# Projecting the first layer's memory values behind the routing instead of in the attention stage

## The chip, the cores and the metric

One core of a Trainium2 chip runs the whole kernel in one launch. The metric is the device time of that launch in microseconds (us). All data are float32.

## The reference

Two blocks run one after the other on 512 tokens of width 1024. The first is a block of sparse attention, a state-space mixer and 16 experts; the second runs two layers (DEPTH_2 = 2), each with a recurrent and windowed-attention mixer, a cross attention to a memory of 256 rows (`mem`), and a swiglu. Cut to what matters here:

```python
def first_block(x, ...):
    att = dsa_attention(q, k, v, iq, ik, iw * INDEXER_SCALE, topk)
    ssd = ssd_mixer(z, xbc, dt_raw, ...)
    mixed = jnp.einsum('bse,ed->bsd', jnp.concatenate([att, ssd], -1), w_out[l])
    x = layer_norm(ALPHA * x + mixed, ln1_g[l], ln1_b[l])
    ffn = hier_moe(x, w_route_group[l], b_route_group[l], w_route_expert[l], ...)
    return layer_norm(ALPHA * x + ffn, ln2_g[l], ln2_b[l])

def hier_moe(h, w_rg, b_rg, w_re, b_re, w_gate, w_up, w_down):
    p_group = jax.nn.softmax((h @ w_rg + b_rg).astype(f32), -1)
    ...
    for e in range(N_EXPERTS):
        hid = jax.nn.silu(h @ w_gate[e]) * (h @ w_up[e])
        y = y + gates[..., e:e + 1] * (hid @ w_down[e])

def cross_attention(u, mem, cq_w, ckv_w, co_w):
    q = (u @ cq_w).reshape(B, S, CROSS_HEADS, CROSS_HEAD_DIM)
    k, v = jnp.split(mem @ ckv_w, 2, axis=-1)
    s = jnp.einsum('bshd,bmhd->bhsm', q, k).astype(jnp.float32) * (CROSS_HEAD_DIM ** -0.5)
    p = jax.nn.softmax(s, axis=-1)
    return jnp.einsum('bhsm,bmhd->bshd', p, v).reshape(B, S, CROSS_WIDTH) @ co_w
```

The product `mem @ ckv_w` of either layer depends on nothing that the first block computes. The kernel computes it early, keeps it in DRAM and reads it back in the layer that uses it.

## The kernel before

**Arithmetic.** A float32 product is made of three matmuls. Each operand is split into a high part (a copy to fp32r on ACT) and a low part (a subtraction on DVE, or on POOL): high x high, high x low, low x high. Tiles named `wh` and `wl` are the two parts of a piece of weights (128 x 1024 elements); `hTh`/`hTl` are those of the activations, transposed; `memh`/`meml` those of the memory.

**Order of the work.** The class `Plan` records every operation of the program first, then lists them in an order of its own: of the operations that are ready by its modelled costs it takes the one that stands first in the program, a little later work filling gaps. Nearly all instructions are therefore issued from one line, L338, and the order on each engine is fixed before the kernel runs; each engine then works through its queue strictly in that order. A `Stream` loads weights in items of 1 MB into two buffers named `raw` (SP issues these loads) and splits them into pieces that go to one of two rings of four, `ring` and `tail` (`take`, L560 to L593). The low part of a piece is made on DVE, except for the keys of the memory and two early projections (L593): those are made on POOL. PSUM banks have three tags with 3, 3 and 2 banks (L208). The projections here use those with tag m.

**The stages around the change**, in the program's order:

- The attention stage: for each of four query blocks `ssd_chunk(i)`, `topk`, `attend(i)` (L1287 to L1291). The scores' softmax, its splits and the products with the values (tiles `pt`, `pth`, `ptl`, `vh`, `vl`) depend on each other, so that PE needs other work in between. `CKV[0]` names such work (L1292): pieces of `ckv`.
- `ckv(l, part)` (L1262 to L1285) projects a part of layer l's memory keys and values. Part "k" makes the keys: eight units of 24 matmuls 128x256, tile `ck`. Parts "0" and "1" make one half of the values each: four pieces of weights, two token tiles, 48 matmuls 128x512, tile `cv`. A result goes from PSUM to an SBUF tile (`kept`, `cko`) and from there to DRAM (`kd`, `vd`).
- The projection `wo` with the norm: 192 matmuls 128x512 in two halves of the columns, four token tiles each; the input x (tile `htokb`, loaded by POOL's queue once the pools of the attention are closed) is added, and the norm's result is transposed to `hTh`, `hTl`.
- The routing: `route()` (the router's matmuls, a long chain of small instructions on DVE, `Lg` to `w`), then for each of the 16 experts its `slots` (a 128x512 comparison on DVE, then eight small matmuls `slot` and `gate` on PE) that give an index list `idx`. `CKV[1]` follows `route()` in the program (L1673).
- The experts: for each of 16, an indirect DMA on POOL's queue gathers its tokens (`xg<-hd,idx`, L1687), PE transposes them (`ps<-ca,xg`), then gate and up (`gu`, 2 MB of weights) and down (1 MB). Three tiles `xg` take the gathers in turn. The loads for several experts run ahead into whatever buffers are free.
- `CKV[2]` follows the experts (L1804). The values of the first layer are read back in the second block, near 985 us.

```python
CKV = (((0, "k"), (0, "0"), (0, "1")), ((1, "k"),), ((1, "0"), (1, "1")))
        plan.critical = True
        route()
        plan.critical = False
        for x in CKV[1]:
            ckv(*x)
```

Of the kernel before, what the change touches and what calls it, by code (L numbers as in the profile page):

```python
# [202 lines left out]
LAT = {"PEACT": 197, "PEDVE": 197, "PEPool": 222, "PEPE": 0, "ACTACT": 153, "ACTDVE": 142, "ACTPE": 271, "ACTPool": 180,  # L203
       "DVEDVE": 127, "DVEACT": 128, "DVEPE": 202, "DVEPool": 153, "PoolPE": 203, "PoolPool": 120}
AHEAD = 50
CKV = (((0, "k"), (0, "0"), (0, "1")), ((1, "k"),), ((1, "0"), (1, "1")))
TABLE_SLACK = 60
PSUM_TAGS = {"m": 3, "c": 3, "s": 2}  # L208
SETS = {}
# [429 lines left out]
def body(tc, a, out):  # L639
# [5 lines left out]
    with ctx:  # L645
# [15 lines left out]
        def bank(name="ps", tag=None):  # L661
            tag = tag or ("c" if name == "ps" else "m")
            return psum.tile([P, 512], F32, tag=tag, name=name, bufs=PSUM_TAGS[tag])
# [60 lines left out]
        def ckv_items(l, part, raws=None, where="ring"):  # L724
            w = a["ckv_w_2"][l]
            if part == "k":
                feat_items(f"ck{l}", w, range(0, 1024))
            else:
                h = int(part)
                tok_items(f"cv{l}{h}", w, K8, 1024 + 512 * h, 512, where, raws=raws)  # L730

        for x in CKV[0]:
            ckv_items(*x)
        for h in range(2):
            tok_items(f"wo{h}", w_out, K8, h * 512, 512,
                      where=("ring", "tail")[h])
        for x in CKV[1]:
            ckv_items(*x)
# [39 lines left out]
        raws = ["raw", "raw", "raw2", "rawb"]  # L778
        for x in CKV[2]:
            ckv_items(*x, raws, "ring")  # L780
# [94 lines left out]
        def feat_mm(p, w, xh, xl, t0=0, t1=NT, kts=K8):  # L875

            wh, wl = w
            n, last = 0, 3 * len(kts) - 1
            o = p[:, t0 * 128:t1 * 128]
            for l, r in ((wh, xh), (wl, xh), (wh, xl)):  # L880
                for k in kts:
                    mm(o, l[:, k, :], r[:, t0:t1, k, :], kts[0] == 0 and n == 0, kts[-1] == 7 and n == last)
                    n += 1

        def tok_mm(p, w, xh, xl, t, kts, n, start, stop):

            wh, wl = w
            c, last = 0, 3 * len(kts) - 1
            for l, r in ((xh, wh), (xh, wl), (xl, wh)):
                for i, k in enumerate(kts):  # L890
                    mm(p[:, :n], l[:, t, k, :], r[:, i, :n], start and c == 0, stop and c == last)
                    c += 1
# [340 lines left out]
        def attend(i):  # L1233
            w = (i + 1) * P
            pts = []
            for pr in range(4):
                ps = pair_scores(hTh[:, i, pr, :], hTl[:, i, pr, :], kTh, kTl, w)
                pt = p3.tile([P, 2, S], F32, tag="pt", name=f"pt{i}_{pr}", bufs=5)[:, :, :w]
                soft_pair(ps, w, acc[i] if i else cmask, 0.125, pt)
                pts.append(pt)  # L1240
            o = None
            for kb in range(i + 1):
                tl = []
                for par in range(2):
                    q = bank()
                    for pr in range(4):
                        T.transpose(q[:, pr * P:(pr + 1) * P], pts[pr][:, par, kb * P:(kb + 1) * P], ident)
                    ph = p3.tile([P, S], F32R, tag="pth", name=f"pth{i}_{kb}_{par}", bufs=2)
                    pl = p3.tile([P, S], F32R, tag="ptl", name=f"ptl{i}_{kb}_{par}", bufs=2)
                    split2(ph, pl, q)  # L1250
                    tl.append((ph, pl))
                if o is None:
                    o = bank()
                for par in range(2):
                    sl = slice(64 * (1 - par), 64 * (1 - par) + 128)
                    ph, pl = tl[par]
                    for n, (l, r) in enumerate(((vh, ph), (vl, ph), (vh, pl))):
                        mm(o, l[:, kb, sl], r, kb == 0 and par == 0 and n == 0, kb == i and par == 1 and n == 2)
            split2(hTh[:, i, 0:4, :], hTl[:, i, 0:4, :], o.rearrange("p (k c) -> p k c", c=P))


        def ckv(l, part):  # L1262
            def kept(m=0):
                if l:
                    return xg[0][:, m // 2 % 2 * 512:m // 2 % 2 * 512 + 512]
                return p3.tile([P, 512], F32, tag="cko", name="cko", bufs=1)
            o = None
            for m in range(8) if part == "k" else ():
                w = st.take((f"ck{l}", m))
                p = bank(f"ck{l}_{m}")  # L1270
                feat_mm(p, w, memh, meml, 0, 2)
                o = o if m % 2 else kept(m)
                plan.copy(o[:, m % 2 * 256:m % 2 * 256 + 256], p[:, :256])
                if m % 2:
                    S_.dma_start(kd[l][:, (m - 1) * 256:(m + 1) * 256], o)
            for h in [int(part)] if part != "k" else ():
                ps = [bank(f"cv{l}_{h}_{t}") for t in range(2)]
                for k in range(0, 8, 2):
                    w = st.take((f"cv{l}{h}", k))
                    for t in range(2):  # L1280
                        tok_mm(ps[t], w, memh, meml, t, [k, k + 1], 512, k == 0, k == 6)
                for t in range(2):
                    o = xg[h][:, t * 512:t * 512 + 512] if l else kept()
                    plan.copy(o, ps[t])
                    S_.dma_start(vd[l][:, t * 1024 + h * 512:t * 1024 + h * 512 + 512], o)  # L1285

        for i in range(4):  # L1287
# [3 lines left out]
            attend(i)  # L1291
        for x in CKV[0]:  # L1292
            ckv(*x)
# [147 lines left out]
        xg = [xgs[:, i * D:i * D + D] for i in range(3)]  # L1441
# [230 lines left out]
# [3 lines that stand above are left out]
# [128 lines left out]
        plan.fence(further)  # L1803
        for x in CKV[2]:  # L1804
            ckv(*x)
# [502 lines left out]
```

## Time and profile before

| what | before |
|---|---|
| median of 3 runs | 2385.21 us (2384.51 to 2388.07) |
| the profiled execution, its own time | 2388.05 us |
| its span, first to last instruction | 2386.3 us |
| mean granted TensorE clock | 0.993 |
| PE busy | 2336.1 us (98%) |
| DVE busy | 1475.7 us (62%) |
| ACT busy | 1146.1 us (48%) |
| POOL busy | 225.7 us (9%) |
| HBM traffic | 275.85 MB read, 20.97 MB written, 124 GB/s over the span |

Busy time is time in which an engine has an instruction under way; matmul ends are modelled, so two matmuls in a row overlap in the rows and the distance of their starts is what one costs. The time between 196 and 505 us of the span holds the stages that the change touches: the last part of the attention (to 248), wo with the norm (to 294), the routing (to 343), the experts (to 505). A row's bracket tells how long the engine was idle before it and what released it. The clock is a share of full speed.

### The profile page before, as it was taken

The page shows a single profiled execution, that of the slowest core. Times are in us where ns is not written, and L with a number is a line of the kernel's source. Part 1 is how long each engine was busy: PE and PEld are TensorE (multiplying, and loading weights), DVE is VectorE, ACT ScalarE, POOL GpSimd, SP SyncE. Part 2 cuts the span into 40 slices and gives each one's busy share as a digit, 9 for nine tenths or more (in the row PEclk, how much of TensorE's full clock was granted, in tenths as well). Part 3 has the DMA queues.
Part 4 walks back from the last instruction along what each step waited for, and adds up shares of the span by engine and source line. Part 5 has one row for each costly group of instructions (what it writes and reads, how often), then busy time and mean ns, then how long its engine had stood idle before and what let it go on. Part 6 is the DMA issues. An engine that isn't in the chain of part 4 may idle for free.

```text
span 2386.3 us, 30257 instructions
## 1 busy us (share of the span) xinstructions
PE 2336.1 (98%) x11681; PEld 1949.3 (82%) x11681; DVE 1475.7 (62%) x2687; ACT 1146.1 (48%) x2004; POOL 225.7 (9%) x214
## 2 busy tenths in 40 slices
PE   9989989989999999999999999999999999999998
PEld 7777777778888888989888888888888888888886
DVE  5987689986883578756333335794477756332334
ACT  5456458756762673544222235673475545322221
POOL 1462532211000000000000001000000000000000
PEclk9999989999999999999999999999999999999999
DMA  6222769984112335322322333213324323232322
GB/s 188 71 85 82 236 205 341 344 300 118 62 62 81 124 104 172 111 71 71 104 91 88 106 106 118 62 54 97 124 80 142 124 94 101 93 103 89 106 80 79
DMA packets 215426, 290.42 MB, mean 122 GB/s; under 512 B 10784, under 2 KB 166640, under 8 KB 214768
## 3 DMA queue, kind: packets, MB, share of 16 engines
q1 hardware_dynamic: 203888, 260.44, 33.5%
q0 software_dynamic: 11392, 28.02, 3.6%
q8 instruction: 92, 1.51, 0.3%
q14 instruction: 54, 0.44, 0.1%
HBM read 275.85 MB, written 20.97 MB: 124 GB/s over the span
## 4 chain that ended last, share of the span: by engine, by line
PE 77%; DVE 1%; ACT 0%; issue 0%; DVEq 0%; ACTq 0%
PE fg L338 10%; PE fu L338 10%; PE fo L338 10%; PE ps L338 6%; PE cq L338 4%; PE bn L338 4%; PE ba L338 4%; PE gn L338 4%; PE q L338 4%; PE co L338 4%; PE wo L338 4%; PE xr L338 4%; PE gr L338 4%; PE ga L338 4%; PE gate L338 2%; PE atto L338 1%
## 5 line engine op out<-in xcount | busy, mean ns | idle before, releaser
L338 DVE TENSOR_TENSOR wl<-raw,wh 128x1024 fp32r<-128x1024 f32 (+1 forms) x390 | 474.8, 1226 | 459.6 <-ACT wh L338 457.7
L338 ACT ACTIVATE wh<-raw 128x1024 fp32r<-128x1024 f32 (+1 forms) x414 | 433.6, 1057 | 570.4 <-PE fu L338 156.5
L324 ACT ACTIVATE lntmp<-ps,lnc 128x128 f32<-128x128 f32 x224 | 85.2, 472 | 45.2 <-PE ps L338 35.1
L338 ACT ACTIVATE fsil<-fg 128x512 f32<-128x512 f32 x44 | 26.3, 598 | 160.1 <-PE fg L338 160.1
L338 DVE TENSOR_TENSOR fsil<-fsil,fu 128x512 f32<-128x512 f32 x44 | 30.2, 687 | 104.9 <-PE fu L338 103.4
L338 PE MATMUL fu<-hTh,wl 128*128 128x512 f32 (+1 forms) x384 | 88.5, 372 | 0.0
L338 PE MATMUL fg<-hTh,wh 128*128 128x512 f32 (+1 forms) x384 | 88.2, 372 | 0.0
L338 PE MATMUL fg<-hTl,wh 128*128 128x512 f32 (+1 forms) x384 | 88.0, 371 | 0.0
L338 PE MATMUL fu<-hTh,wh 128*128 128x512 f32 (+1 forms) x384 | 88.0, 371 | 0.0
L338 PE MATMUL fg<-hTh,wl 128*128 128x512 f32 (+1 forms) x384 | 88.0, 371 | 0.0
L338 PE MATMUL fu<-hTl,wh 128*128 128x512 f32 (+1 forms) x384 | 88.0, 371 | 0.0
L338 PEld LDWEIGHTS fu<-hTh,wl 128*128 128x128 f32 x384 | 68.4, 188 | 12.4
L338 PEld LDWEIGHTS fu<-hTh,wh 128*128 128x128 f32 x384 | 68.3, 188 | 12.5
L338 PEld LDWEIGHTS fg<-hTh,wl 128*128 128x128 f32 x384 | 68.3, 188 | 12.5
L338 PEld LDWEIGHTS fu<-hTl,wh 128*128 128x128 f32 x384 | 68.3, 188 | 12.5
L338 PEld LDWEIGHTS fg<-hTl,wh 128*128 128x128 f32 x384 | 68.3, 188 | 12.4
L338 PEld LDWEIGHTS fg<-hTh,wh 128*128 128x128 f32 x384 | 68.2, 188 | 12.3
L338 ACT ACT_TABLE_LOAD x53 | 68.0, 1283 | 11.6 <-DVE c_mx L338 5.2
L338 PE MATMUL gu<-wh,hTm 128*128 128x512 f32 x256 | 72.4, 394 | 1.0 <-DVE hl L338 1.0
L338 POOL TENSOR_TENSOR wl<-raw,wh 128x1024 fp32r<-128x1024 f32 x24 | 58.1, 2427 | 105.6 <-ACT wh L338 105.5
L338 DVE TENSOR_TENSOR htokL<-htokL,lngb 128x512 f32<-128x512 f32 x96 | 63.0, 677 | 0.0
L338 ACT ACTIVATE pt<-pt,a_nb 128x256 f32<-128x256 f32 (+1 forms) x128 | 59.8, 472 | 1.6 <-DVE a_nb L338 1.6
(606 smaller groups left out, 5700.4 us busy)
## 6 DMA issues: line engine op xcount, KB each, us to landing
raw<-in_w_in_dram SPq DMA_DIRECT2D x47, 1024.0 KB, 5.3
raw<-in_ffn_wi_dram SPq DMA_DIRECT2D x44, 1024.0 KB, 5.1
raw<-in_ffn_wo_dram SPq DMA_DIRECT2D x20, 1024.0 KB, 5.0
raw<-in_ckv_w_dram SPq DMA_DIRECT2D x15, 1024.0 KB, 5.5
raw<-in_w_out_dram SPq DMA_DIRECT2D x12, 1024.0 KB, 5.0
raw<-in_w_down_dram SPq DMA_DIRECT2D x8, 1024.0 KB, 7.5
raw<-in_w_br_attn_dram SPq DMA_DIRECT2D x8, 1024.0 KB, 4.9
raw<-in_w_br_rnn_dram SPq DMA_DIRECT2D x8, 1024.0 KB, 5.0
```

The lines of the kernel that those rows point to most:

```text
L324: "ACT": (lambda: act.activation(out.real(), src.real(), AF.Identity, bias=bias.real(), scale=scale.real()), 0.836 * n + 235, 0.0)}
L338: return getattr(eng.real, method)(*[f(x) for x in args], **{k: f(x) for k, x in kw.items()})
```

## The change

The table `CKV` moves the two halves of the first layer's values from the first group (the attention) to the second, behind the second layer's keys. `kept` then gives the values of either layer a slice of `xg[0]` for their way to DRAM; `cko`, a tile of the attention's pool `p3`, stays with the first layer's keys. The loads of the weights move with it, since the lists of loads are built from the same table.

```diff
-CKV = (((0, "k"), (0, "0"), (0, "1")), ((1, "k"),), ((1, "0"), (1, "1")))
+CKV = (((0, "k"),), ((1, "k"), (0, "0"), (0, "1")), ((1, "0"), (1, "1")))
...
             def kept(m=0):
-                if l:
+                if l or part != "k":
                     return xg[0][:, m // 2 % 2 * 512:m // 2 % 2 * 512 + 512]
                 return p3.tile([P, 512], F32, tag="cko", name="cko", bufs=1)
...
                 for t in range(2):
-                    o = xg[h][:, t * 512:t * 512 + 512] if l else kept()
+                    o = xg[h][:, t * 512:t * 512 + 512] if l else kept(2 * t)
                     plan.copy(o, ps[t])
                     S_.dma_start(vd[l][:, t * 1024 + h * 512:t * 1024 + h * 512 + 512], o)
```

**PE at the end of the attention stage.** `cv_1_0` is the second half of the values, first token tile; `wo_0` the projection's first token tile. Before, the last query block:

```order
L338 MATMUL ps<-pth_1_0_2575,vl 128x512
L338 MATMUL cv_1_0_2468<-wh_2525,meml 128x512
L338 MATMUL cv_1_1_2487<-wh_2525,memh 128x512 x2
L338 MATMUL ps<-ptl_1_0_2585,vh 128x512
L338 MATMUL ps<-pth_1_1_2581,vh 128x512
```

and with the change:

```order
L338 MATMUL ps<-ca,pt_3_2416 128x128
L338 MATMUL ps<-pth_3_0_2573,vh 128x512
L338 MATMUL ps<-pth_3_0_2573,vl 128x512
L338 MATMUL ps<-ptl_3_0_2579,vh 128x512
L338 MATMUL ps<-pth_3_1_2577,vh 128x512
L338 MATMUL ps<-pth_3_1_2577,vl 128x512
L338 MATMUL ps<-ptl_3_1_2583,vh 128x512
L338 MATMUL wo_3_2654<-wh_1863,hTh 128x512 x2
```

The token tiles `wo_0`, `wo_1` and `wo_2` of the projection's first half now stand between the attention's earlier instructions, where `cv` stood; the last query block has nothing between its own, and behind it comes `wo_3`.

**PE ahead of the first expert.** `gu` is the first expert's gate and up. Before:

```order
L338 MATMUL gate<-rg,slots 128x3
L338 MATMUL ps<-ca,xg 128x128 x8
L338 MATMUL gu_3674<-wh_3072,hTm 128x512
L338 MATMUL ps<-ca,xg 128x128 x4
L338 MATMUL gu_3674<-wh_3072,hTm 128x512
```

and with the change (the first row has the slots of eleven experts ahead of it):

```order
L338 MATMUL cv_0_0_3556<-wh_3530,memh 128x512 x2
...
L338 MATMUL cv_0_1_3573<-wl_3571,memh 128x512 x2
L338 MATMUL cv_0_1_3573<-wh_3552,meml 128x512 x2
L338 MATMUL ps<-ca,xg 128x128 x12
...
L338 MATMUL cv_1_1_3714<-wh_3726,memh 128x512 x2
L338 MATMUL cv_1_1_3714<-wl_3738,memh 128x512 x2
L338 MATMUL cv_1_1_3714<-wh_3726,meml 128x512 x2
L338 MATMUL ps<-ca,xg 128x128 x4
L338 MATMUL gu_3790<-wh_2992,hTm 128x512 x2
```

All 96 matmuls of `cv` stand between the slots of the eleventh expert and the first `gu`; 24 of them stand ahead of the transposes of the first gather.

**POOL around the first gather.** `wl` are the low parts of the second layer's keys. Before:

```order
L338 TENSOR_TENSOR wl_3220<-raw_2939,wh_3200 128x1024
L338 TENSOR_TENSOR wl_3283<-raw_2939,wh_3266 128x1024
L338 TENSOR_TENSOR wl_3314<-raw_2997,wh_3298 128x1024
L338 TENSOR_TENSOR wl_3415<-raw_2997,wh_3388 128x1024
...
L1687 DMA xg<-hd,idx 128x1024 x6
```

and with the change:

```order
L338 TENSOR_TENSOR wl_3128<-raw_2849,wh_3025 128x1024
L338 TENSOR_TENSOR wl_3160<-raw_2849,wh_3115 128x1024
...
L1687 DMA xg<-hd,idx 128x1024
L338 TENSOR_TENSOR wl_3395<-raw_3134,wh_3376 128x1024
L338 TENSOR_TENSOR wl_3427<-raw_3134,wh_3393 128x1024
L1687 DMA xg<-hd,idx 128x1024 x6
```

Two of the keys' eight splits on POOL now stand behind the first gather.

## Rows read from the trace of the kernel before

**Rows 1.** The page's part 1: busy time, share, instructions of each engine.

```profile
PE 2336.1 (98%) x11681; PEld 1949.3 (82%) x11681; DVE 1475.7 (62%) x2687; ACT 1146.1 (48%) x2004; POOL 225.7 (9%) x214
```

**Rows 2.** Stage table: stretch, length; busy (instructions) of each engine; clock, DMA share, GB/s.

```profile
196.00:248.00 52.00, 52.00 (x261) 40.14 (x260) 36.63 (x91) 34.59 (x65) 7.45 (x6) 1.00 0.32 108
248.00:294.00 46.00, 44.13 (x205) 36.27 (x204) 27.00 (x42) 19.98 (x36) 28.40 (x23) 1.00 0.81 246
294.00:343.00 49.00, 38.68 (x318) 35.56 (x316) 43.47 (x86) 24.00 (x47) 18.67 (x13) 0.88 0.61 208
343.00:505.00 162.00, 152.85 (x801) 125.02 (x801) 150.53 (x200) 123.08 (x167) 43.39 (x43) 0.99 0.93 318
```

**Rows 3.** Tile cv, 190 to 260 us: duration ns min/median/max, first and last start.

```profile
L338 PE MATMUL cv<-wh,memh x32: 387/393/501, 196.1 to 239.5; 128*128 128x512 f32 x32
```

**Rows 4.** Timeline of PE, 240 to 250 us: start, us, instruction [idle before <-releaser].

```profile
242.43 0.39 PE L338 MATMUL wo<-wh,hTh 128*128 128x512 f32 x1
...
247.85 0.39 PE L338 MATMUL ps<-ptl,vh 128*128 128x512 f32 x1
...
248.76 0.62 PE L338 MATMUL wo<-wh,hTh 128*128 128x512 f32 x2
249.21 0.61 PE L338 MATMUL wo<-wl,hTh 128*128 128x512 f32 x2
```

**Rows 5.** Groups by line, 196 to 248 us: busy us, mean ns, idle before.

```profile
L338 DVE TENSOR_TENSOR wl<-raw,wh 128x1024 fp32r<-128x1024 f32 x9 | 10.9, 1222 | 3.9 <-ACT wh L338 3.9
...
L338 ACT ACTIVATE wh<-raw 128x1024 fp32r<-128x1024 f32 x9 | 9.4, 1052 | 0.3 <-PE cv L338 0.3
```

**Rows 6.** Timelines of DVE and POOL behind the attention's end.

```profile
252.06 0.13 DVE L338 MEMSET rv<- 128x16 bf16 x3 [2.46 <-DMA vd<-cko]
...
252.55 2.16 POOL L338 DMA_DIRECT2D htokb<-in_x_dram  x4 [33.56 <-DMA raw<-in_w_gate_dram]
...
259.41 0.54 POOL L338 DMA_DIRECT2D cm<-in_c_m_dram  x1 [1.82 <-DMA htokb<-in_x_dram]
```

**Rows 7.** Timeline of PE, norm's first transposes and the routing's start.

```profile
281.16 1.09 PE L338 MATMUL ps<-ca,htokb 128*128 128x128 f32 x8 [1.87 <-DVE htokb L338]
...
294.37 1.18 PE L338 MATMUL route<-hTh,wrh 128*20 128x256 f32 x8
```

**Rows 8.** Timeline of DVE in the routing.

```profile
314.83 4.17 DVE L338 TENSOR_TENSOR wl<-xg,wh 128x1024 fp32r<-128x1024 f32 x2
...
327.18 2.37 DVE L338 TENSOR_SCALAR den<-ex 128x4 f32<-128x4 f32 x1 [0.70 <-ACT ex L338]
...
331.76 1.41 DVE L338 TENSOR_TENSOR slots<-cm,px 128x512 bf16<-128x512 f32 x2
...
334.46 0.14 DVE L338 TENSOR_SCALAR idx<-idx 128x1 int32<-128x1 int32 x1
...
335.40 1.89 DVE L338 TENSOR_TENSOR slots<-cm,px 128x512 bf16<-128x512 f32 x3
```

**Rows 9.** Timeline of PE in the routing, and the first expert's first matmul.

```profile
319.66 1.04 PE L338 MATMUL route<-hTl,wrh 128*20 128x256 f32 x4 [4.39 <-DVE hTl L338]
...
342.85 0.80 PE L338 MATMUL gu<-wh,hTm 128*128 128x512 f32 x1
```

**Rows 10.** Timeline of POOL in the routing.

```profile
327.13 2.39 POOL L338 TENSOR_TENSOR wl<-raw,wh 128x1024 fp32r<-128x1024 f32 x1 [10.34 <-ACT wh L338]
...
334.88 1.10 POOL L1687 DMA_INDIRECT xg<-hd,idx  x1 [2.27 <-DVE slotv L338]
```

**Rows 11.** DMA issues, 180 to 420 us: count, KB each, median us to landing.

```profile
raw<-in_ckv_w_dram SPq DMA_DIRECT2D x5, 1024.0 KB, 5.8
...
xg<-hd,idx POOLq DMA_INDIRECT x12, 6.9
```

**Rows 12.** Table by stretches, columns as in group 2.

```profile
320.00:322.00 2.00, 2.00 (x11) 1.77 (x9) 0.41 (x1) 0.00 (x0) 0.00 (x0) 0.50 0.70 137
```

**Rows 13.** Tile slots on DVE, columns as in group 3.

```profile
L338 DVE TENSOR_TENSOR slots<-cm,px x16: 679/683/795, 331.8 to 427.7; 128x512 bf16<-128x512 f32 x16
```

## The prediction

> **What bounds the kernel now.** I read the page's totals first, then a table of the stages around the change, then the rows in the timelines at each stage's ends, then the groups by tile and the DMA issues. TensorE (PE) is busy for 98% of the span [rows 1], so the first question of any edit is what it does to PE's gaps. The stage table [rows 2] shows where those gaps are: none in the last part of the attention (196 to 248 us, 52.00 of 52.00 busy), 1.9 us in the projection wo with its norm (248 to 294), 10.3 us in the routing (294 to 343, clock 0.88), 9.2 us in the expert stage (343 to 505). The attention's end is gapless because the first layer's memory values, tile cv, are its filler: three kinds of cv matmul, 32 of each, of which one group starts between 196.1 and 239.5 [rows 3]. The routing is a chain of small steps on DVE, POOL and DMA, and PE waits in it. The change takes the filler from a place without gaps to a place that has them, which sounds like a gain. The question is whether cv can stand in those gaps.
>
> I call "no change" what lies within 0.2% (4.8 us), about what a measurement of this kernel can tell. The rows come from an execution of 2388.05 us whose span is 2386.3; the median of the runs is 2385.21, 2.8 lower. I add the sum to 2388.05 for the profile and to the median for the forecast.
>
> **1. The attention loses its filler (gain 4 us, 0 to 7.4).** Two matmuls 128x512 of the projection start 0.45 us after the two before [rows 4], so one costs 0.225 and the 96 of cv 21.6 us. In the new order three of the four token tiles of wo's first half, 72 matmuls, become the filler, where so far 9 of wo's matmuls ran, from 242.43 on, before the last attention matmul at 247.85 [rows 4]. The stage holds 96 + 9 - 72 = 33 fewer, worth 7.4 us at most. But the new order leaves no filler at all in the last query block, and there PE waits for the softmax's splits on ACT and DVE. At worst each matmul taken out leaves a hole: 0. I take the middle, 4.
>
> cv's eight pieces also leave ACT and DVE here, 1.05 and 1.22 us each by the rows of nine in this stage [rows 5], but wo's splits for the same buffers move up in their place, so these engines gain little. Four stores of cv leave SP's queue; the last holds a DVE instruction back by 2.46 us at 252.06 [rows 6]. That wait goes, and the loads of htokb behind it on POOL move up with the attention's end.
>
> **2. The tail from the attention's end to the routing (gain 10 us, 6 to 14.3).** Now it is 46.5 us from the start of the last attention matmul to the first route matmul at 294.37 [rows 4, 7]. Left are 120 of wo's 192 matmuls, 27.0 us, three groups of eight transposes at 1.09 each, 3.3, and the stall of 1.87 in front of the first of them [rows 7]: 32.2 us, a gain of 14.3 if nothing else is late. What is late next is htokb. Its loads were issued at 252.55 and the first had landed by 259.41 [rows 6], 6.9 us, and only then can a finished token tile leave its PSUM bank. Before, wo had only begun when those loads were issued. Now three banks are full when the attention ends, the fourth tile's 24 matmuls give 5.4 us of cover, and then the second half needs a bank: 6.9 - 5.4 = 1.5 us of waiting, and by my estimate as much again twice, 3, until the evacuations and the last norm on DVE have caught up. 14.3 - 4.5 is 10. If that doubles, 6 is left.
>
> Parts 1 and 2 together can't pass the 21.6 us of PE work that left.
>
> **3. The routing's chain (gain 3 us, 0 to 6.5).** In the new order the two DVE splits of an expert's weights, 4.17 us at 314.83 [rows 8], stand behind the last hTl of the routing and no longer ahead of it; PE waited 4.39 us for that hTl [rows 9]. And a split on POOL of 2.39 us, beside which a DVE instruction on 128x4 took 2.37 [rows 8, 10], leaves the stretch between the router's result and the slots. Both gone: 6.5. Something else usually comes last then (ck's splits are now later on POOL), so half of it.
>
> **4. The way to the first expert (loss 24 us, 14.9 to 27.4).** This is the term that decides. Now the first index list is ready at 334.46, its gather is issued at 334.88, and the first expert matmul starts at 342.85 [rows 8, 9, 10]: 8.4 us. Between them PE has the last memory keys of layer 1 to do and hardly waits. In the new order all 96 cv matmuls stand between the index list and the first expert, in a queue that PE takes strictly in order:
> - The first cv matmul comes behind the slots of eleven experts. Six slot instructions of DVE took 331.76 to 337.29 with their small ones, 0.92 each [rows 8]; three are done when the index list is, eight are left: 7.4 us. On top of it POOL now has two of the keys' splits behind the gather (2.39 each), and DVE instructions beside such a split end with it [rows 8, 10], up to 4.8 more. I take 9.
> - 96 matmuls: 21.6 us.
> - The other slots and gathers' transposes, 1.0 and 1.0 us.
> That gives the first expert 32.6 us after the index list, 24 later than now. The loads say nearly the same: the second of cv's four items of weights waits for a buffer that POOL's two late splits free, 0.4 + 1.1 + 4.8 after the index list; a load of this kind lands in 5.8 us [rows 11]; a split on ACT and DVE 2.3; the fourth item can be loaded only then, again 5.8 + 2.3; its 24 matmuls take 5.4; some 2 more for the transposes: 30. So neither a faster PE nor a faster queue alone would shorten it. The bounds: if nothing waits and only the matmuls that the gather doesn't cover count (it takes 6.9 us to land [rows 11], so 30 of 96 are hidden), 66 x 0.225 = 14.9; with all of the 7.4 + 4.8 ahead of the first cv matmul, 3.2 more than I take, 27.4.
>
> The clock can add to it. After the wait of 4.39 us PE runs at 0.50, the lower of its two levels, in 320 to 322 [rows 9, 12]. I put that into the upper rival.
>
> **5. The expert stage (0, -4 to +4).** PE, DVE and the DMA are all nearly full there [rows 2], and the weights ahead of it fill all their buffers before the first expert in either order, so a later start is carried through. Against it stands that 10 of 16 slot instructions of 0.68 us [rows 13], which now run in that stage (six are named above), are nearly all done before it; for it, that the third expert's gather must wait until the values, which now go through the same tile, are stored. I let them cancel. The later stages are untouched: the values are read back only in the second block's first cross attention.
>
> **Sum:** -4 - 10 - 3 + 24 + 0 = +7. Profile 2395, median **2392**.
>
> A page of the Trainium skill bears on part 4: "Perfetto Trace Analysis", section "Optimizing Scalar/DVE Operations", says GPSIMD and DVE share an SBUF read port, so moving work between those two may not help. This trace agrees as far as the pair of 2.37 and 2.39 us goes; taken to the letter the slots would lose the whole 4.8 us, and the sum would be about +10.
>
> **The rivals.**
> - **A, the routing swallows cv (faster, about 2379).** PE has 10.3 us of gaps and a low clock in the routing [rows 2]. If about half of cv stands in them or beside the gather, only 48 matmuls, 10.8 us, lie ahead of the first expert: -4 - 10 - 3 + 10.8 = -6. It decides where more than 20 of the 96 run before the index list, or where parts 1 and 2 reach 20 us. For it: the gaps are real. Against it: the new order puts every cv matmul behind the slots of eleven experts, after the gaps. The Trainium skill's "Perfetto Trace Analysis", section "Optimization Strategy", speaks for this one: interleaving regimes whose most contended engine differs may help. No row here shows that it does.
> - **B, it cancels (about 2383).** The change does not remove a matmul; it shifts 21.6 us of them. If part 4 comes to its lower bound, because no load and no split is late: -4 - 10 - 3 + 14.9 = -2. For it: PE is the engine without gaps nearly everywhere else. Against it: the load chain above, 30 us by itself.
> - **C, worse (about 2403).** While cv waits for loads in small bursts the clock stays at its lower level for half of it: 48 x 0.225 = 10.8 on top, +18. It needs waits like the 4.39 us one [rows 9], and those come from POOL's late splits.
> That the change doesn't do what it says is half true already: its values stand behind the routing's chain, not in it.
>
> **How the numbers follow.** Forecast 0.47, A 0.20, B 0.25, C 0.08. Slower is the forecast and C, 0.55; of B nearly all lies within 4.8 us, 0.24; A gives faster, 0.21. The range runs from A's time, 2378, to just under C's, 2402, and leaves out a tenth at either end.
>
> **What would show it.** Right: the route matmuls start about 14 us earlier; the gap from the index list to the first expert matmul grows from 8.4 to some 32 us, with cv gapless or in bursts inside; the length from there to the end of the experts is unchanged within 4 us. Part 1 is wrong if PE in the attention's last part is idle by more than 5 us, part 2 if PE waits over 3 us for htokb. The prediction fails as a whole if many cv matmuls start before the index list is ready, or if the expert stage gets shorter by 8 us because it has fewer slots and fuller buffers.

## The result, and the profile after

The changed kernel takes 2404.32 us (median of 4 runs, 2403.06 to 2404.64), the kernel before beside it 2385.76: a ratio of 1.0068 (95% interval 1.0052 to 1.0083), **slower by 0.7%**. The two profiled executions differ by 16.5 us in their own times (2404.58 and 2388.05) and in their spans (2402.8 and 2386.3). The forecast was slower by 7 us; the median lies just above the top of the range (2402), and the ratio, applied to the 2385.2 that the forecast started from, gives 2401 to 2402, just inside.

The page's part 1 of the changed kernel, against [rows 1]:

```profile
PE 2342.7 (98%) x11681; PEld 1951.3 (81%) x11681; DVE 1481.0 (62%) x2685; ACT 1148.2 (48%) x2006; POOL 216.7 (9%) x214
```

The number of PE instructions is the same; nothing was added, the work moved. Where the time went is seen from five marks on PE and DVE: the last attention matmul, the first route matmul, the first index list, the first expert matmul (`gu`) and the experts' last (`dn`). The timeline of PE after, with the columns of [rows 4]:

```profile
241.68 0.40 PE L338 MATMUL ps<-ptl,vh 128*128 128x512 f32 x1
...
279.68 1.94 PE L338 MATMUL ps<-ca,htokb 128*128 128x128 f32 x8 [6.69 <-DVE htokb L338]
281.27 2.05 PE L338 MATMUL route<-hTh,wrh 128*20 128x256 f32 x8
...
323.00 0.24 PE L338 MATMUL slot<-rv,slots 128*128 128x2 bf16 x3 [5.57 <-DVE slots L338]
...
325.29 2.05 PE L338 MATMUL ck<-memh,wl 128*128 128x256 f32 x8
...
333.57 0.72 PE L338 MATMUL cv<-wh,memh 128*128 128x512 f32 x2
...
360.22 0.71 PE L338 MATMUL gu<-wh,hTm 128*128 128x512 f32 x2
```

The attention ends 6.2 us earlier, the routing starts 13.1 us earlier than in [rows 7], and the first expert starts 17.4 us later than in [rows 9]. The timelines of DVE and POOL around the first index list tell why, against [rows 8, 10]:

```profile
316.12 0.15 DVE L338 TENSOR_SCALAR idx<-idx 128x1 int32<-128x1 int32 x1
...
316.87 5.49 DVE L338 TENSOR_SCALAR idx<-idx 128x2 int32<-128x2 int32 x1
322.27 1.88 DVE L338 TENSOR_TENSOR slots<-cm,px 128x512 bf16<-128x512 f32 x3
```

```profile
316.54 1.11 POOL L1687 DMA_INDIRECT xg<-hd,idx  x1 [3.11 <-DVE slotu L338]
317.68 4.64 POOL L338 TENSOR_TENSOR wl<-raw,wh 128x1024 fp32r<-128x1024 f32 x2
```

A DVE instruction on 128 x 2 numbers started while POOL issued the gather and ended with POOL's second split of the keys: 5.49 us. Its six sisters need 0.15 to 0.17 (tile `idx` in the changed kernel: least, median and longest time in ns):

```profile
L338 DVE TENSOR_SCALAR idx<-idx x7: 146/167/5487, 316.1 to 367.2; 128x3 int32<-128x3 int32 x4, 128x1 int32<-128x1 int32 x2, 128x2 int32<-128x2 int32 x1
```

By the profile no instruction waited for a result of these splits; PE waited for the slots behind the held instruction (5.57 us) and then ran at a low clock. The stage table after, columns as in [rows 2]:

```profile
242.00:281.00 39.00, 30.68 (x144) 25.45 (x144) 29.43 (x42) 17.71 (x33) 22.89 (x20) 0.95 0.71 207
281.00:316.00 35.00, 29.21 (x228) 26.42 (x227) 32.60 (x64) 20.31 (x43) 19.12 (x11) 0.91 0.68 224
316.00:323.00 7.00, 1.43 (x20) 1.23 (x17) 7.00 (x13) 2.16 (x4) 6.12 (x4) 0.66 0.80 300
323.00:334.00 11.00, 10.03 (x106) 9.43 (x106) 5.93 (x17) 3.62 (x6) 0.85 (x1) 0.75 0.38 131
334.00:339.00 5.00, 4.67 (x21) 3.43 (x20) 5.00 (x13) 0.00 (x0) 0.00 (x0) 0.66 0.31 80
339.00:360.20 21.20, 21.20 (x115) 17.56 (x114) 12.74 (x14) 10.48 (x14) 1.00 (x1) 1.00 0.64 212
360.20:523.00 162.80, 152.44 (x736) 123.11 (x735) 143.93 (x176) 122.71 (x166) 31.64 (x42) 0.99 0.94 320
```

From 316 to 323 PE is busy for 1.43 us of 7; from 323 to 339 its clock is 0.66 to 0.75; then the values run gapless at 1.00, with the gather's transposes among them.

The same stretches in all profiled executions, each from the start times of the marks in its own timeline (us; "rest" reaches to the second block's first matmul for q):

| kernel | attention to route | route to index list | index list to first expert | experts | rest |
|---|---|---|---|---|---|
| before | 46.5 | 40.1 | 8.4 | 163.5 | 46.5 |
| changed | 39.6 | 34.9 | 44.1 | 163.7 | 45.5 |
| e8_two_keys_on_DVE | 39.4 | 34.9 | 36.7 | 163.4 | 45.7 |
| e3_keys_low_on_DVE | 36.7 | 30.0 | 32.1 | 163.9 | 45.4 |
| e9_idle_work_on_POOL | 36.5 | 30.3 | 37.2 | 164.1 | 45.2 |
| e2_hi_only | 39.4 | 35.0 | 31.5 | 173.0 | 47.9 |
| e1_half | 40.7 | 38.3 | 23.7 | 165.1 | 45.4 |
| e4_behind_experts | 39.6 | 34.8 | 20.6 | 170.1 | 63.8 |
| e5_before_keys_on_DVE | 45.7 | 32.4 | 7.2 | 166.8 | 46.6 |
| e6_half_keys_on_DVE | 38.8 | 29.1 | 19.8 | 166.6 | 45.3 |
| e7_behind_experts_keys_on_DVE | 36.3 | 30.7 | 8.9 | 162.6 | 63.2 |
| e10_behind_experts_DVE_rows | 31.3 | 30.2 | 13.3 | 163.6 | 63.2 |
| e11_half_DVE_rows | 34.2 | 28.0 | 20.7 | 163.6 | 45.5 |
| e12_before_DVE_rows | 44.9 | 28.7 | 10.4 | 163.1 | 46.8 |

The index list is not a fixed place in PE's queue. Of the 192 matmuls of the second layer's keys, 0.12 us each at the full clock, 48 stand between the index list and the first expert in the changed kernel, e2, e4 and e8, 38 in the kernel before, 37 in e1, 19 in e3 and e9, 17 in e7, 51 in e10, and 31 to 42 in the rest. Two kernels can be compared in this stretch as they stand only where this number is the same; 30 more of them make it 3.6 us longer.

### The profile page after: what moved, and what is told of

It reads as the page before. It is cut to its first block, busy times and chain, and to the rows that moved or that the text cites. A ratio compares the mean times of both kernels' runs of the same rounds, so it can differ in the third digit from the quotient of the medians.

```text
span 2402.8 us, 30235 instructions
## 1 busy us (share of the span) xinstructions
PE 2342.7 (98%) x11681; PEld 1951.3 (81%) x11681; DVE 1481.0 (62%) x2685; ACT 1148.2 (48%) x2006; POOL 216.7 (9%) x214
## 4 chain that ended last, share of the span: by engine, by line
PE 91%; DVE 6%; ACT 1%; issue 1%; DMA 1%; SPq 0%; DVEq 0%; ACTq 0%
PE fg L338 10%; PE fu L338 10%; PE fo L338 9%; PE ps L338 8%; PE wo L338 5%; PE q L338 5%; PE cq L338 4%; PE bn L338 4%; PE ba L338 4%; PE gn L338 4%; PE co L338 4%; PE xr L338 4%; PE gr L338 4%; PE ga L338 4%; PE gu L338 2%; PE gate L338 2%
## 5 line engine op out<-in xcount | busy, mean ns | idle before, releaser
L324 ACT ACTIVATE lntmp<-ps,lnc 128x128 f32<-128x128 f32 x224 | 85.6, 471 | 49.9 <-PE ps L338 40.7
L338 DVE TENSOR_TENSOR fsil<-fsil,fu 128x512 f32<-128x512 f32 x44 | 30.3, 688 | 104.9 <-PE fu L338 103.4
L338 DVE TENSOR_TENSOR htokL<-htokL,lngb 128x512 f32<-128x512 f32 x96 | 63.2, 678 | 0.0
L338 PE MATMUL wo<-wh,hTh 128*128 128x512 f32 x192 | 60.8, 396 | 1.6 <-ACT hTh L338 1.6
```

Source lines behind the costliest of these rows:

```text
L324: "ACT": (lambda: act.activation(out.real(), src.real(), AF.Identity, bias=bias.real(), scale=scale.real()), 0.836 * n + 235, 0.0)}
L338: return getattr(eng.real, method)(*[f(x) for x in args], **{k: f(x) for k, x in kw.items()})
```

## The experiments

Theory 1 at the outset: PE takes its queue in order, so the values ahead of the first expert count in full, and POOL's two late key splits delay the slots ahead of them. Its rivals: the chain of loads sets that way, or the loss lies in the expert stage. Each ratio is against runs of the kernel before on the same chip.

### First four: how much stands ahead of the first expert, and why

**e1_half**, one half of the values back in the attention:

```diff
-CKV = (((0, "k"),), ((1, "k"), (0, "0"), (0, "1")), ((1, "0"), (1, "1")))
+CKV = (((0, "k"), (0, "0")), ((1, "k"), (0, "1")), ((1, "0"), (1, "1")))
-                if l or part != "k":
+                if l or part == "1":
```

> One half of the first layer's values goes back into the attention stage, the other half stays behind the second layer's keys. Theory 1 (PE works through its queue in order, and what stands ahead of the first expert counts in full, with the slots delayed by POOL's late key splits): 48 matmuls are left ahead of the first expert, 10.8 us instead of 21.6, and in this order all key splits stand ahead of the first gather, so the 5.5 us DVE instruction on the index list is gone: from index list to first expert 20 to 25 us instead of 44.1; the attention and the tail keep half of their gain. Time 2391 (2387 to 2396). Theory 2 (the chain of loads through two buffers sets the way to the first expert): two loads are left instead of four, 8 to 16 us less of 44, 2393 to 2400. A theory that the loss lies in the expert stage itself (values through the gathers' tile): no shorter way to the first expert, above 2398.

Measured: 2395.32 us, ratio 1.0034 (1.0022 to 1.0047); index list to first expert 23.7 us. Half of the values, half of the loss, and the way shrank by 20.4, more than the 10.8 of the matmuls: all key splits stand ahead of the first gather here.

**e2_hi_only**, 32 of 96 matmuls:

```diff
-                        tok_mm(ps[t], w, memh, meml, t, [k, k + 1], 512, k == 0, k == 6)
+                        if l:
+                            tok_mm(ps[t], w, memh, meml, t, [k, k + 1], 512, k == 0, k == 6)
+                        else:
+                            for j in range(2):
+                                mm(ps[t], memh[:, t, k + j, :], w[0][:, j, :], k + j == 0, k + j == 7)
```

> The changed kernel, but of the 96 matmuls of the first layer's values only the 32 of high x high are made; the loads and the splits stay. It leaves out the two low products. Theory 1 (PE's queue): 64 x 0.225 = 14.4 us less between index list and first expert, 44.1 to about 30, time about 2390 (2387 to 2394). Theory 2 (loads and splits set it): 44.1 shortens by 4 us at most, 2400 to 2404.

Measured: 2402.11 us, ratio 1.0063 (1.0041 to 1.0085). The time speaks for theory 2. In the trace the first expert starts 12.6 us sooner behind its index list, near the 14.4 of theory 1, but only 20 of the 32 value matmuls stand ahead of it, and the experts then take 173.0 us and not 163.7. Timeline of PE:

```profile
345.57 0.39 PE L338 MATMUL gu<-wh,hTm 128*128 128x512 f32 x1
...
359.62 0.69 PE L338 MATMUL hidT<-ca,sg 128*128 128x128 f32 x2 [5.71 <-DVE sg L338]
```

With fewer matmuls the planner listed the work anew, and the activation of the first expert's `gu` on ACT came behind the weight splits of later pieces; PE waited for it. A run that changes what the planner counts also changes the order, so this one settles nothing about the price of the matmuls. Theory 2 falls by the changed kernel's own rows: from the first value matmul to the first expert PE waits 0.33 us in all. So does the theory of the expert stage: the experts take 163.7 us there, 163.5 before.

**e3_keys_low_on_DVE**, no split of these keys on POOL:

```diff
-        (self.G if key[0] in ("z", "q", "ck0", "ck1") else self.V).tensor_sub(parts[1], src, parts[0].bitcast(F32))
+        (self.G if key[0] in ("z", "q", "ck0") else self.V).tensor_sub(parts[1], src, parts[0].bitcast(F32))
```

> The changed kernel with the low parts of the second layer's keys made on DVE and no longer on POOL: no POOL split stands behind the first gather. Theory 1 with its part on POOL and DVE: the DVE instruction of 5.5 us on the index list falls to 0.2, PE's wait of 5.6 us before the third slot goes, and the first value matmul comes 8 to 11 us after the index list instead of 17.5; against it DVE has 8 x 1.2 = 9.8 us more to do, most of it ahead of the index list. Time 2397 (2393 to 2403). If POOL's splits don't hold DVE up, only the added work is left: 2406 to 2414.

Measured: 2385.68 us (10 runs), ratio 0.9985 (0.9975 to 0.9995). Against the changed kernel's 1.0068 that is 0.83%, some 20 us, from eight splits of 2.3 to 3.4 us on an engine that is busy for 9% of the span. All three stretches ahead of the first expert shrink: by 2.9, 4.9 and 12.0 us; 3.5 of the 12.0 are the 29 key matmuls that now stand ahead of the index list. The effect was expected, its size not (7 us).

**e4_behind_experts**:

```diff
-CKV = (((0, "k"),), ((1, "k"), (0, "0"), (0, "1")), ((1, "0"), (1, "1")))
+CKV = (((0, "k"),), ((1, "k"),), ((0, "0"), (0, "1"), (1, "0"), (1, "1")))
```

> The first layer's values go behind the experts, ahead of the second layer's values: nothing of them in the attention or the routing. Theory 1: the start of the routing and the index list keep the gain of the change (13 and 18 us earlier than before), the way from index list to first expert is 8.4 plus what POOL's two late key splits cost, 14 to 18, so the first expert starts 8 to 12 us earlier than before; behind the experts 96 matmuls are added, of which 2 to 6 us stand in gaps: +16 to +20. Time 2393 (2388 to 2397). If the way to the first expert stays above 30 us without the values, theory 1 is wrong, and the time is above 2402.

Measured: 2401.85 us, ratio 1.0055 (1.0036 to 1.0073), 9 us above what was expected. With no value in it the way to the first expert takes 20.6 us, against 8.4 before: 12.2 us more. The changed kernel's hold is there again (`idx` on 128 x 2 takes 5.49 us, PE then waits 5.57), but not all of the 12.2 need be the two late splits': ten more key matmuls, 1.2 us, stand there too. And the rest of the head start, 5.9 us at the first expert, was lost in the experts, which take 170.1 us. Two stretches of its stage table:

```profile
337.00:350.00 13.00, 10.23 (x70) 8.49 (x68) 10.10 (x26) 7.62 (x9) 2.98 (x3) 0.76 0.54 173
350.00:360.00 10.00, 9.64 (x41) 7.63 (x39) 5.30 (x7) 5.74 (x8) 0.99 (x1) 0.75 0.46 126
```

PE is nearly full from 350 to 360 at a granted clock of 0.75. The kernel before in the same stretches:

```profile
337.00:350.00 13.00, 11.67 (x83) 10.12 (x83) 10.82 (x17) 7.74 (x11) 1.85 (x3) 0.87 0.58 194
350.00:360.00 10.00, 9.30 (x76) 7.56 (x75) 10.00 (x17) 7.75 (x12) 4.83 (x4) 1.00 0.78 251
```

### Next four: the values' place without POOL's splits

**e5_before_keys_on_DVE** is the kernel before with the edit of e3, **e6_half_keys_on_DVE** is e1 with it, **e7_behind_experts_keys_on_DVE** is e4 with it. **e8_two_keys_on_DVE** is the changed kernel with this one:

```diff
-        (self.G if key[0] in ("z", "q", "ck0", "ck1") else self.V).tensor_sub(parts[1], src, parts[0].bitcast(F32))
+        (self.G if key[0] in ("z", "q", "ck0") or key[0] == "ck1" and key[1] < 6 else self.V).tensor_sub(parts[1], src, parts[0].bitcast(F32))
```

> The kernel before, with the low parts of the second layer's keys on DVE instead of POOL. Theory A (POOL's splits hold DVE up wherever they run, and that was the larger part of the changed kernel's loss): here all eight stand ahead of the first gather, PE waits for DVE 1.9, 3.2 and 4.4 us beside them, and DVE gets 9.8 us more to do: a small gain, 2380 (2375 to 2385), and then the change without POOL's splits (2385.7) costs about 5 us by itself. Theory B (the changed place gains by itself and only POOL's late splits hid it): no gain here, 2386 to 2392, above the changed kernel with the keys on DVE.

Measured: 2380.96 us, ratio 0.9977 (0.9965 to 0.9989). The time is theory A's forecast; the 5 us that it left to the change by itself are 0.08% (2 us) in the ratios.

> One half of the first layer's values in the attention, the other behind the keys, and the keys' low parts on DVE. Theory A: between the kernel before and the changed one, both with the keys on DVE, 2383 (2378 to 2388). Theory B: the more values behind the keys the better, 2386 to 2389.

Measured: 2380.45 us, ratio 0.9969 (0.9956 to 0.9982). Theory A had it between e5 and e3; it lies below both, by less than the intervals can tell.

> The first layer's values behind the experts, and the keys' low parts on DVE. Theory A: from index list to first expert 8 to 11 us instead of 20.6, no low clock behind it, so that the head start over the kernel before, 15 to 20 us at the index list, reaches the first expert; if the experts keep their length of 163.5 us it reaches their end, and 18 us of values behind them give 2384 (2379 to 2390). If the experts' end doesn't move (the loads' pace sets it, not their start), 2396 to 2402.

Measured: 2381.88 us, ratio 0.9972 (0.9961 to 0.9983). The way to the first expert is 8.9 us, the experts keep their length (162.6), and the head start reaches their end. Their first matmul, in PE's timeline:

```profile
318.10 0.79 PE L338 MATMUL gu<-wh,hTm 128*128 128x512 f32 x1
```

The values then cost 16.7 us behind the experts (63.2 - 46.5), less than their 21.6.

So with the keys on DVE four places of the values give 0.9977 (attention), 0.9969 (half), 0.9985 (routing) and 0.9972 (behind the experts), with intervals that overlap. The change by itself is worth 0.08%, which these runs can't tell from nothing; with POOL's splits it costs 0.68%.

> The changed kernel with only the last two of the keys' eight low parts on DVE, those that stood on POOL behind the first gather. Theory A: from index list to first expert 44.1 shrinks to 32 to 34, as with all eight on DVE; the stretch ahead of the index list stays. Time 2393 (2390 to 2397), about 11 us less than the changed kernel and 8 more than with all eight on DVE. If the late pair isn't special, a quarter of the 19 us that all eight bring: 2399.

Measured: 2397.19 us, ratio 1.0040 (1.0026 to 1.0054), between the two cases. The late pair is worth 7.4 us on the way to the first expert, a third of the whole. This is its cleanest price, since 48 key matmuls stand there in both kernels; the expected 32 to 34 us were not reached for the same reason, as e3 has 19. The other six splits work on the stretches ahead of the index list, 2.7 and 4.9 us longer than in e3. The timelines of POOL, DVE and PE: the gathers follow each other, the `idx` that was held takes 0.16 us, and the first value matmul comes 9.8 us behind the index list (313.79):

```profile
314.21 1.10 POOL L1687 DMA_INDIRECT xg<-hd,idx  x1 [3.20 <-DVE slotu L338]
315.62 1.70 POOL L1687 DMA_INDIRECT xg<-hd,idx  x1 [0.30 <-DVE slots L338]
```

```profile
314.54 0.16 DVE L338 TENSOR_SCALAR idx<-idx 128x2 int32<-128x2 int32 x1
```

```profile
323.59 1.18 PE L338 MATMUL cv<-wh,memh 128*128 128x512 f32 x4
```

### Last four: is it the hold on DVE, and what beats both

**e9_idle_work_on_POOL** is e3 with two POOL operations that nobody waits for:

```diff
+                V.tensor_scalar(one, gate[:, 0:1], 0.0, 1.0, op0=OP.mult, op1=OP.add)
+                for _ in range(2):
+                    G.tensor_tensor(htok[0], htok[0], one.to_broadcast([P, D]), op=OP.mult)
```

> The changed kernel with the keys' low parts on DVE, plus two multiplications 128x1024 on POOL behind the first index list (a norm row by one, nobody waits for them before the experts are done). It separates the two ways in which POOL's late splits can cost: Theory A (a tensor operation on POOL holds up the DVE instructions that start beside it): a DVE instruction behind the index list takes 2 to 5 us, index list to first expert grows from 32.1 to 35 to 39, time 2389 to 2393. Theory C (PE waited for the results of the late splits, and DVE's length was only a symptom): no change, 2385 to 2387.

Measured: 2389.71 us, ratio 1.0005 (0.9994 to 1.0016); e3 had 0.9985. The way to the first expert grows from 32.1 to 37.2 us, with 19 key matmuls in either. DVE in e9, then POOL:

```profile
312.33 6.39 DVE L338 TENSOR_TENSOR slots<-cm,px 128x512 bf16<-128x512 f32 x4
```

```profile
312.50 2.26 POOL L338 TENSOR_TENSOR htokb<-htokb,one 128x1024 f32<-128x1024 f32 x1 [2.18 <-DVE one L338]
314.92 1.31 POOL L1688 DMA_INDIRECT xg<-hd,idx  x1 [0.16 <-issue]
316.26 1.90 POOL L338 TENSOR_TENSOR htokb<-htokb,one 128x1024 f32<-128x1024 f32 x1
```

and the same four slots on DVE in e3, with nothing on POOL beside them:

```profile
320.19 2.49 DVE L338 TENSOR_TENSOR slots<-cm,px 128x512 bf16<-128x512 f32 x4
```

6.39 against 2.49 us. Two operations on POOL whose results no other instruction needs there cost 5.1 us, the late pair 7.4 (e8): in e9 it is the hold on DVE and not the wait for a result. For the six splits ahead of the index list no run separates the two; the trace of the changed kernel shows no instruction that waits for any of the eight.

**e10_behind_experts_DVE_rows**, **e11_half_DVE_rows** and **e12_before_DVE_rows** are e7, e6 and e5 with the norm rows' multiplications on DVE:

```diff
-                norm_rows(t, gb, G if 3 >> t & 1 else V)
+                norm_rows(t, gb, V)
```

> The first layer's values behind the experts, the keys' low parts on DVE, and the norm rows' multiplications, so far on POOL for two of four token tiles, all on DVE too: no tensor operation of POOL from the attention's end to the slots but the gates' small ones. Theory A: the wait of 3 us of PE before the norm's transposes shrinks to 1 or 2 and the DVE instructions there fall back to 0.7, at a price of 4 x 1.2 us on DVE: 2379 (2374 to 2383) beside 2381.9. If POOL's rows don't matter: 2382 to 2386.

Measured: 2379.9 us, ratio 0.9967 (0.9954 to 0.9979): no gain that its interval tells from e7. In the attention-to-route stretch it won 5.0 us, on the way to the first expert it lost 4.4; 4.1 of these are 34 more key matmuls behind the index list (51 against 17), work put off and not a wait.

> As the run before, with one half of the first layer's values in the attention and the other behind the keys. Theory A: 2378 (2374 to 2382) beside 2380.5; if POOL's rows don't matter, 2381 to 2384.

Measured: 2373.51 us, ratio 0.9942 (0.9928 to 0.9955). **This version beats both kernels**, by 13.7 us against the kernel before beside it, a little more than was expected.

> As the two runs before, with the values in the attention as in the kernel before. Theory A: 2379 (2374 to 2383) beside 2381.0, and all three places of the values within 5 us of each other once POOL does no tensor work there. If the place matters by itself, this one or the one behind the experts stands out by more than 5 us.

Measured: 2375.56 us, ratio 0.9958 (0.9945 to 0.9972). The values' place matters a little here: half and half lies 6.4 us below behind the experts, where theory A had all three within 5. Moving the rows gained 0.27% for half and half (e11 against e6), 0.19% here (against e5) and 0.05% behind the experts, which is within the noise; no run shows why it differs.

## Why the prediction was right, and where it was off

The direction, the place and the term that decides came out as forecast. The size did not: +16.6 us where +7 was forecast, and most of the difference lies in one term. By the parts, from the marks:

- **1, the attention:** -4 forecast, -6.2 measured (247.85 to 241.68). PE lost 0.25 us at a time in the last query block, 0.75 from 196 to 242, not a hole for every matmul.
- **2, the tail:** -10 forecast, -6.9 measured (46.5 to 39.6). The cause that was named, banks waiting for htokb's loads, did not occur: PE runs without a gap from 243.70 to the last wo matmul at 272.38. Late was the norm: PE waited 6.69 us for it, and by the sign that the prediction gave (more than 3 us for htokb) this part was wrong. Its DVE work stood behind a `hTl` that took 5.42 us beside POOL's norm rows. The same hold that decided part 4, then, has no term in part 2. DVE and POOL there:

```profile
271.89 5.42 DVE L338 TENSOR_TENSOR hTl<-lntmp,hTh 128x512 fp32r<-128x512 f32 x1
```

```profile
272.09 4.66 POOL L338 TENSOR_TENSOR htokb<-htokb,lngb 128x1024 f32<-128x1024 f32 x2
```

- **3, the routing's chain:** -3 forecast, -5.2 measured (40.1 to 34.9). Both named delays went: PE's wait for the last hTl is 0.88 us and the `den` of 2.37 takes 0.17. Something else came in their place, as the prediction allowed: PE waits 4.32 us for a norm beside three key splits on POOL (287.09 to 296.51).
- Together -18.3 where -17 was forecast; the errors cancel.
- **4, the way to the first expert:** +24 forecast, **+35.7** measured (8.4 to 44.1). This is the step that was mis-sized, in the sentence "On top of it POOL now has two of the keys' splits behind the gather ..., up to 4.8 more. I take 9." The first value matmul came 17.5 us after the index list, not 9: 8.5 of the 11.7 us that the part was off. Without the late pair it came after 9.8 (e8), so that the pair cost 7.7 us there, where the sum had 1.6 beside the 7.4 of the slots: the hold of 5.49 in full, then rows of eight key matmuls that take 2.05 us and not 1.12, and slots that PE's order put behind those keys. From the first value matmul to the first expert it took 26.7 us, where the sum had 23.6; the first values ran at a clock of 0.66 (334 to 339). That e8's 9.8 lies so near the 9 is partly luck. There PE has 48 key matmuls to do in that time, 5.8 us at 0.12 each, for which the sum has no term; in e3, with 19 of them, the first value matmul came after 5.8 us. The values' own share was right: e3 against e7, 32.1 - 8.9 = 23.2 us, and the changed kernel against e4, 44.1 - 20.6 = 23.5, where the sum has 24 less the 1.6.
- **5, the experts:** 0 forecast, +0.2 measured; later stages -1.0.

-6.2 - 6.9 - 5.2 + 35.7 + 0.2 - 1.0 = +16.6, the 16.5 of the spans.

The Trainium skill's "Perfetto Trace Analysis", section "Optimizing Scalar/DVE Operations", taken to the letter, gave an estimate of +10 and was nearer than the forecast's +7. The Trainium skill's "SBUF — State Buffer", section "SBUF: two separate sides", says more: the shared pair of ports is an exclusive lock, and of a POOL instruction and a DVE instruction in a two-port mode, or with two SBUF inputs against a POOL instruction that reads SBUF, the first to start has it for the whole instruction, while the other fully blocks. The 5.49 us of `idx` and e9's 6.39 us agree in that the DVE row lasts until POOL's work is done; that `idx` was blocked through two POOL instructions in a row the sentence does not say, and that these ports are the cause no run here shows.

**The rivals.** A (the routing swallows the values) fell: no value matmul ran before 333.57. B (it cancels) fell with the same 44.1 us. C gave 2403, and its time is nearer than the forecast's 2392. Its condition occurred, a wait like the 4.39 us one from POOL's late splits (5.57 us). Its mechanism did not: the values did not wait for loads in bursts and ran at 1.00 from 339 on; the low clock was on the keys and the first values.

e8's way to the first expert is 4.6 us longer than e3's although no split stands behind the gather in either: 3.5 of these are 29 more key matmuls behind its index list. What stays open is the other 1.1, and which of the six earlier splits costs what.

## What to carry to other kernels

Before work is moved past a chain of small vector instructions, look at what POOL will be doing beside that chain: here the move cost 0.7% with eight tensor operations on POOL, and without them nothing that can be measured. Work split over DVE and POOL can lose on a chain that PE waits for. When a move trades equal work between two places, read the gain ahead of the wait and the loss behind it separately: what starts earlier gains nothing if more work then stands in the queue. And before a stretch between two marks is compared across kernels, count what other work stands in it.

## What the runs showed of the hardware that was not expected

- By the rows, the hold began while POOL issued an indirect DMA (the DVE instruction started at 316.87, the gather's issue ran from 316.54 to 317.65) and went through the two tensor operations behind it. The issue by itself does not hold DVE: in e8, with no tensor operation behind the gather, the same instruction started at the same point of the issue (314.54, the issue from 314.21 to 315.31) and took 0.16 us.
- The stretch from 152 to 200 us, ahead of nearly everything that these edits move, ran at two clocks: 0.96 in the kernel before, the changed one, e4, e7 and e8, and 0.75 in e3 and e5. No run shows why. The stage table there, in the kernel before and in e3:

```profile
152.00:200.00 48.00, 44.00 (x273) 34.66 (x273) 37.33 (x108) 30.13 (x72) 26.29 (x22) 0.96 0.20 65
```

```profile
152.00:200.00 48.00, 44.03 (x225) 33.86 (x224) 31.14 (x83) 22.80 (x55) 23.17 (x19) 0.75 0.19 61
```

In e3's profiled execution the attention ended some 9 us later than in the changed kernel (250.61 against 241.68); that execution took 2393.53 us, the longest of the kernel's ten, whose median is 2385.68. For this reason stretches between marks are compared above, and times by medians.
